# Storing and reloading split weights for the second half of the tokens in a hybrid RWKV-7 / S5 layer

## The chip, the cores and the metric

The kernel runs on one core of one Trainium2 chip. The metric is the device time of one execution in microseconds (us). Three runs of the kernel before gave a median of 1566.11 us (1561.93 to 1569.23). One more execution was recorded by the hardware profiler; all views of the profile are of that one.

## What is computed

One layer of a decoder trunk, in float32, for 1024 tokens of width 1024. The first sub-layer mixes tokens by two branches in parallel, an RWKV-7 recurrence and an S5 state-space scan, and merges them by learned gates:

```python
gates = sigmoid(h @ w_in[..., gate columns] + b_gate); g_rwkv, g_s5 = split(gates, 2)
# S5 branch, its last step
y = gelu(y); y = y * sigmoid(y @ w_glu + b_glu)
# merge of the branches, output projection, residual
o_rwkv = rwkv7_branch(...) @ w_branch_rwkv        # 512 -> 1024
o_s5   = s5_branch(...)    @ w_branch_s5          # 512 -> 1024
mixed  = (g_rwkv * o_rwkv + g_s5 * o_s5) @ w_out  # 1024 -> 1024
x = x + rms_norm(mixed, norm_mix_post)
```

The second sub-layer is a gated MLP with a short convolution. The change does not touch it.

## The kernel before

**Three matmuls for one.** TensorE multiplies in a rounded float32 type. To keep accuracy, each operand is split into a rounded part (names that end in `h`: `wh`, `hh`) and the remainder (`wl`, `hl`), and `mm3_steps` (L163) makes three matmuls for each 128x128 block of weights: `wh`·`xh`, `wh`·`xl`, `wl`·`xh` (L173, L174, L175). Activations are 128 features by 512 tokens, so the tokens fall in two halves, first and second (`th` 0 and 1 in the code).

**Weights.** `load_w` (L144) loads a 128x512 tile of weights into `wf` (L156, 256 KB, issued on SyncE's queue), rounds it into `wh` on ScalarE (L157), and takes the remainder into `wl` on VectorE (L158). There are two `wf` buffers and four each of `wh` and `wl` in rotation. So the load of a tile waits until the tile two before has been rounded and subtracted, and the rounding of a tile waits until TensorE is done with the tile four before. A weight of 512 inputs (`w_glu`, `w_br`) is one such tile; one of 1024 inputs (`w_out`, `w_up`) is two.

**The merge.** For either half of the tokens there are 4 tiles of `w_glu` (`glu_tile`, L1073), 16 of `w_br` (`gate`, L1084; for each block of 128 outputs one tile for RWKV and one for S5) and 16 of `w_out` (`outproj`, L1215): 36 tiles. `glu_tile` reads the S5 output `YU` again for its last product (L1064, packets of 256 bytes); `gate` reads the stored gates `GT` (L1088) and multiplies them with the matmul result on VectorE (L1091). For the first half this work (`merge`, `outproj(0)`) is background work, which `drive` (L186) puts between the steps of the RWKV recurrence. For the second half, `merge_s5` does the four `glu` tiles and the S5 gates, `merge_rk` the RWKV gates and the sums, and `outproj(1)` the projection. Beside the latter runs `mid_norms(0)`: the first half's post-norm (L1202, L1203, with `x` loaded again into `tx`, L1194), the stores of the sum (`X`, L1206), its squares, and the pre-norm of the MLP (L1252).

**Order.** TensorE's instructions stay in the order in which the code emits them. On all other engines and on SyncE's queue a scheduler orders them by priority and by its own estimate of when each is ready; `load_w` has a high priority (`HPW`). Each engine, and SyncE's queue too, then runs its list strictly in that order: an instruction that waits holds up all behind it.

Of the kernel before, what the change touches and what calls it, by code (L numbers as in the profile page):

```python
# [9 lines left out]
F32 = mybir.dt.float32  # L10
# [61 lines left out]
class Kern:  # L72
# [68 lines left out]
            V.scalar_tensor_tensor(y, h, 1.5, y, ALU.add, ALU.mult)  # L141
        return y

    def load_w(self, *srcs, pool=None):  # L144

        nc = self.nc
        wh, wl = [], []
        wp = pool or self.wp
        with self.tc.high_priority(HPW):
            for src in srcs:  # L150
                for o in range(0, src.shape[1], 512):
                    n = min(512, src.shape[1] - o)
                    h = wp.tile([128, 512], F32R, tag="wh", name=self.nm("wh"), bufs=4 if pool else NWH)
                    l = self.lx() if pool else wp.tile([128, 512], F32R, tag="wl", name=self.nm("wl"), bufs=NWL)
                    f = self.wp.tile([128, 512], F32, tag="wf", name=self.nm("wf"), bufs=NWF)
                    nc.sync.dma_start(f[:, :n], src[:, o:o + n])  # L156
                    nc.scalar.copy(h[:, :n], f[:, :n])  # L157
                    nc.vector.tensor_tensor(l[:, :n], f[:, :n], h[:, :n].bitcast(F32), ALU.subtract)  # L158
                    wh.append(h)
                    wl.append(l)  # L160
        return wh, wl

    def mm3_steps(self, ps, w, wk, xh, xl):  # L163
# [909 lines left out]
    def glu_tile(self, m, xs, t, y, to):  # L1073

        nc = self.nc
        w = self.load_w(self.a["w_glu"][m])
        ps = self.gmp()
        yield from self.mm3_steps(ps, w, 0, [x[0] for x in xs], [x[1] for x in xs])
        t3 = t.rearrange("p (n j) -> p n j", j=8)
        nc.scalar.activation(t, ps, AF.Tanh, bias=self.hb["b_glu"][:, m:m + 1], scale=0.5)  # L1080
        nc.vector.scalar_tensor_tensor(t3, t3, 1.0, y(), ALU.add, ALU.mult)
        self.split_half(*to, t)

    def gate(self, j, m, th, br, t, out):  # L1084

        nc = self.nc
        w = self.load_w(self.a["w_br"][j, m])
        nc.sync.dma_start(t, self.GT[8 * j + m][:, th * 512:th * 512 + 512])  # L1088
        ps = self.gmp()
        yield from self.mm3_steps(ps, w, 0, [b[0] for b in br], [b[1] for b in br])  # L1090
        nc.vector.scalar_tensor_tensor(out, t, 1.0, ps, ALU.add, ALU.mult)  # L1091
# [123 lines left out]
    def outproj(self, th, mg, mx):  # L1215

        nc, hp = self.nc, self.hp[th]
        for m in range(NK):
            w = self.load_w(self.a["w_out"][m])
            ps = self.gmp()  # L1220
            yield from self.mm3_steps(ps, w, 0, [x[0] for x in mg], [x[1] for x in mg])
            y = hp.tile([128, 512], F32, tag=f"hl{m}", name=self.nm("mx"), bufs=1)
            nc.scalar.copy(y, ps)
            mx.append(y)
            sq = hp.tile([128, 512], F32, tag=f"hh{m}", name=self.nm("sq"), bufs=1)
            nc.scalar.activation(sq, y, AF.Square)
            if m:
                nc.vector.tensor_tensor(sq, sq, self.acc[th], ALU.add)
            self.acc[th] = sq
# [479 lines left out]
    def front_half(self):  # L1709

        tc = self.tc
        self.h = [None, None]
        self.now = self.credit = 0.0
        self.pause, self.fill_prio, self.acc = False, HPW, {}
        self.mark, self.chained = False, False
        self.s5_in_done, self.stored, self.mixed_in, self.open = -1, None, False, 0
        with tc.tile_pool(name="lxp", bufs=4) as self.lxp, tc.tile_pool(name="s5c", bufs=1) as self.s5c, \
                tc.tile_pool(name="u8p", bufs=1) as u8p, tc.tile_pool(name="eva", bufs=NEVA) as self.evp, \
                tc.tile_pool(name="psx", bufs=1, space=PSUM) as self.psx:
            self.ps, self.ngm = self.psx, 4  # L1720
            self.u8 = [u8p.tile([128, 8, 128], F32, name=f"u8_{b}") for b in range(4)]
            with tc.tile_pool(name="xp", bufs=1) as xp:
                with tc.high_priority(HPN):
                    xs = [self.load_x(0, xp)]
                    self.setup()
                    self.s5w = {}
                    self.s5_load(0)
                    self.s5_load(1)
                    for _ in self.norm(0, xs[0], xp):
                        pass  # L1730
                    xs.append(self.load_x(1, xp))
                self.fill = [self.s5_in(xp), self.mix_in()] + [self.gate_tiles(m) for m in range(14)] + [
                    self.merge_loads(), self.gate_tiles(14, 15)]
                self.outs, self.yr = 0, []
                self.drive([(HPN, self.norm(1, xs[1], xp))])
                self.drain(lambda: self.stored == 3)
                with tc.high_priority(HP):
                    self.s5_setup()
            with tc.tile_pool(name="s5p", bufs=1) as self.s5p:
                self.s5d = [{} for _ in range(4)]  # L1740
                self.tabs = self.s5_done = -1
                self.drive([(HP, self.s5_lane()), (HP, self.tab_lane())])
                self.drain(lambda: self.mixed_in and not self.open)
        self.early_stack = ExitStack()
        self.rka = self.early_stack.enter_context(tc.tile_pool(name="rka", bufs=1, side="right"))
        with tc.tile_pool(name="rk", bufs=1) as self.rk, tc.tile_pool(name="evb", bufs=NEV) as self.evp, \
                tc.tile_pool(name="psy", bufs=1, space=PSUM) as self.psx:
            self.ps, self.ngm = self.psx, 2
            self.rwkv_setup()
            self.ds = [{} for _ in range(4)]  # L1750
            self.nat = self.prep = self.chains = -1
            self.fronts = 0
            mg, self.mx0 = [], []
            self.drive([(HP, self.prep_lane(0)), (HP, self.prep_lane(1)), (HP2, self.chain_lane()), (HP2, self.out_lane(mg))])
            self.drain(lambda: self.mark)
# [148 lines left out]
```

## Time and profile before

| | |
|---|---|
| median of three runs | 1566.11 us (1561.93 to 1569.23) |
| profiled execution, its own time | 1569.72 us |
| its span in the trace | 1566.6 us |
| TensorE busy | 1490.2 us, 95% of the span, mean granted clock 0.977 |
| VectorE busy | 1127.4 us, 72% |
| ScalarE busy | 691.0 us, 44% |
| DMA | 213.84 MB, 137 GB/s over the span |

A page of the profile gives busy times of engines, the groups of instructions that cost most, and the DMA issues with the time from issue to landing. "PE" is TensorE, "DVE" VectorE, "ACT" ScalarE, "POOL" GpSimd, "SPq" SyncE's DMA queue. In a row of the timeline stand the start in us, the duration in us, the engine, the line, the operation, what it writes and reads, and in brackets how long the engine was idle before it and what ended that. A table of windows gives the busy time of PE, its weight loads, DVE, ACT and POOL for each stretch of the span, the granted clock (1.00 is full speed), the mean busy share of the 16 DMA engines, and what they moved in GB/s. In the second half of the tokens the `glu` tiles start near 757 us, the S5 gates at 770 us, the RWKV gates at 802.6 us and the projection at 824.4 us, which ends near 881 us.

### The profile page before, as it was taken

What the parts mean: (1) busy time and instruction counts of PE and PEld (TensorE: products, weight loads), DVE (VectorE), ACT (ScalarE), POOL (GpSimd) and SP (SyncE); (2) the same over time, 40 slices, a digit from 0 to 9 for tenths busy, and PEclk for the clock granted to TensorE, in tenths of its full rate; (3) what the DMA queues carried; (4) which work ended last, traced back from release to release, by engine and by line L of the source; (5) the groups of instructions that cost most, each with busy time, mean ns of one, the idle gap of its engine ahead of it and who ended that gap; (6) DMA issues with size and microseconds to landing.
All of it is one profiled execution on the core that took longest, in us unless ns stands there. A gap on an engine that the chain in (4) does not pass through costs nothing.

```text
span 1566.6 us, 26064 instructions
## 1 busy us (share of the span) xinstructions
PE 1490.2 (95%) x10028; PEld 1194.1 (76%) x10028; DVE 1127.4 (72%) x1963; ACT 691.0 (44%) x1115; POOL 164.2 (10%) x218
## 2 busy tenths in 40 slices
PE   5999899999999999999998999999999999999995
PEld 4787788787777776667686888788888887888784
DVE  6798784664465656875586689877777777698777
ACT  5354442224243345565433445444445444443451
POOL 2120000415224142100000000000000000000000
PEclk9999999999999989999898999999999999999997
DMA  6164243344335256552854343322222225943712
GB/s 210 41 201 124 85 126 124 110 137 145 109 116 159 84 172 169 142 163 79 264 189 158 133 165 135 114 88 81 82 81 81 81 84 197 321 171 121 241 68 107
DMA packets 133420, 213.84 MB, mean 137 GB/s; under 512 B 38656, under 2 KB 44800, under 8 KB 133296
## 3 DMA queue, kind: packets, MB, share of 16 engines
q1 hardware_dynamic: 124208, 188.32, 36.4%
q0 software_dynamic: 7936, 21.77, 4.7%
q10 hardware_dynamic: 1152, 2.10, 0.3%
q8 instruction: 78, 1.28, 0.3%
q14 instruction: 46, 0.38, 0.1%
HBM read 156.56 MB, written 53.48 MB: 134 GB/s over the span
## 4 chain that ended last, share of the span: by engine, by line
PE 71%; DVE 14%; DMA 7%; issue 4%; ACT 3%; SPq 1%; POOL 1%; DVEq 0%; ACTq 0%; POOLq 0%
PE gm L173 9%; PE gm L174 8%; PE gm L175 8%; PE rp L1344 4%; PE rp L1345 4%; PE rp L1346 4%; DMA st<-in_w_down_dram 2%; PE ch L173 2%; PE ch L174 2%; PE mm L174 2%; PE mm L1346 2%; PE mm L1345 2%; PE ch L175 2%; PE mm L1344 2%; PE mm L173 2%
## 5 line engine op out<-in xcount | busy, mean ns | idle before, releaser
L173 PE MATMUL gm<-hh,wh 128*128 128x512 f32 x688 | 294.1, 428 | 5.5 <-ACT hh L227 2.1
L174 PE MATMUL gm<-hl,wh 128*128 128x512 f32 x688 | 273.1, 397 | 0.4 <-DVE hl L228 0.4
L175 PE MATMUL gm<-hh,wl 128*128 128x512 f32 x656 | 259.9, 396 | 0.0
L157 ACT CAST wh<-wf 128x512 fp32r<-128x512 f32 x179 | 110.8, 619 | 209.7 <-PE gm L174 125.7
L158 DVE TENSOR_TENSOR wl<-wf,wh 128x512 fp32r<-128x512 f32 x175 | 123.9, 709 | 97.5 <-ACT wh L157 82.7
L173 PEld LDWEIGHTS gm<-hh,wh 128*128 128x128 f32 x688 | 131.3, 191 | 42.4 <-issue 4.3
L174 PEld LDWEIGHTS gm<-hl,wh 128*128 128x128 f32 x688 | 131.8, 192 | 23.8 <-issue 1.4
L175 PEld LDWEIGHTS gm<-hh,wl 128*128 128x128 f32 x656 | 125.0, 191 | 28.1
L1519 PE MATMUL d<-xl,wh 128*128 128x512 f32 x308 | 120.9, 393 | 3.4 <-DVE xl L228 3.4
L1518 PE MATMUL d<-xh,wh 128*128 128x512 f32 x308 | 120.7, 392 | 2.1 <-ACT xh L227 2.1
L1520 PE MATMUL d<-xh,wl 128*128 128x512 f32 x308 | 120.6, 392 | 0.0
L1344 PE MATMUL rp<-t,h 128*128 128x512 f32 x216 | 84.4, 391 | 1.4 <-ACT p L1358 1.4
L1346 PE MATMUL rp<-t,l 128*128 128x512 f32 x216 | 84.2, 390 | 0.5 <-DVE l L228 0.5
L1345 PE MATMUL rp<-t,h 128*128 128x512 f32 x216 | 84.1, 389 | 0.0
L1519 PEld LDWEIGHTS d<-xl,wh 128*128 128x128 f32 x308 | 58.2, 189 | 17.0 <-DVE xl L228 5.1
L1518 PEld LDWEIGHTS d<-xh,wh 128*128 128x128 f32 x308 | 58.2, 189 | 14.6 <-ACT xh L227 2.4
L1520 PEld LDWEIGHTS d<-xh,wl 128*128 128x128 f32 x308 | 58.1, 189 | 12.1
L227 ACT CAST h<-r 128x1024 fp32r<-128x1024 f32 x34 | 35.8, 1054 | 61.1 <-PE rp L1345 32.5
L228 DVE TENSOR_TENSOR l<-r,h 128x1024 fp32r<-128x1024 f32 x34 | 41.6, 1225 | 29.3 <-ACT h L227 27.8
L1365 DVE SCALAR_TENSOR_TENSOR y<-zv,vecs,y 128x1023 f32<-128x1023 f32 (+1 forms) x36 | 46.1, 1281 | 8.6 <-ACT y L1363 8.6
L1344 PEld LDWEIGHTS rp<-t,h 128*128 128x128 f32 x216 | 40.5, 188 | 10.8 <-ACT p L1358 2.2
L1346 PEld LDWEIGHTS rp<-t,l 128*128 128x128 f32 x216 | 40.5, 188 | 9.3 <-DVE l L228 1.0
(442 smaller groups left out, 3373.0 us busy)
## 6 DMA issues: line engine op xcount, KB each, us to landing
r<-in_w_up_dram SPq DMA_DIRECT2D x36, 512.0 KB, 3.2
wf<-in_w_in_dram SPq DMA_DIRECT2D x68, 256.0 KB, 2.7
st<-in_w_down_dram SPq DMA_DIRECT2D x55, 256.0 KB, 4.3
st<-ACT SPq DMA_DIRECT2D x44, 256.0 KB, 4.5
wf<-in_w_up_dram SPq DMA_DIRECT2D x36, 256.0 KB, 2.8
ACT<-y POOLq DMA_DIRECT2D x18, 512.0 KB, 2.9
GT<-ev SPq DMA_DIRECT2D x32, 256.0 KB, 2.1
wf<-in_w_br_dram SPq DMA_DIRECT2D x32, 256.0 KB, 3.1
```

The source lines that it names most:

```text
L157: nc.scalar.copy(h[:, :n], f[:, :n])
L158: nc.vector.tensor_tensor(l[:, :n], f[:, :n], h[:, :n].bitcast(F32), ALU.subtract)
L173: mm(ps, a, xh[k], start=k == 0, stop=False)
L174: mm(ps, a, xl[k], start=False, stop=False)
L175: mm(ps, b, xh[k], start=False, stop=k == n - 1)
L1344: mm(ps, wh[:, c], xh, start=first and k == 0, stop=False, skip_group_check=True)
L1345: mm(ps, wh[:, c], xl, start=False, stop=False, skip_group_check=True)
L1346: mm(ps, wl[:, c], xh, start=False, stop=k == 3, skip_group_check=True)
L1365: V.scalar_tensor_tensor(y[:, lag:], z[:, 0:1024 - lag], self.vec(nme, i), y[:, lag:], ALU.mult, ALU.add)
L1518: mm(ps, wh[:, c], xh[:, x], start=start, stop=False, skip_group_check=True)
L1519: mm(ps, wh[:, c], xl[:, x], start=False, stop=False, skip_group_check=True)
L1520: mm(ps, wl[:, c], xh[:, x], start=False, stop=stop, skip_group_check=True)
```

## The change

When a tile of `w_glu`, `w_br` or `w_out` is made for the first half of the tokens, `wh` and `wl` are also stored to DRAM (256 KB each). The stores are issued by the next call of `load_w`. When the same tile is asked for again, both parts are loaded straight into `wh` and `wl`, and neither `wf` nor the rounding nor the subtraction is there.

```diff
-    def load_w(self, *srcs, pool=None):
+    def load_w(self, *srcs, pool=None, key=None):
...
+        new = []
         with self.tc.high_priority(HPW):
             for src in srcs:
                 for o in range(0, src.shape[1], 512):
                     n = min(512, src.shape[1] - o)
                     h = wp.tile([128, 512], F32R, tag="wh", name=self.nm("wh"), bufs=4 if pool else NWH)
                     l = self.lx() if pool else wp.tile([128, 512], F32R, tag="wl", name=self.nm("wl"), bufs=NWL)
+                    wh.append(h)
+                    wl.append(l)
+                    if (key, o) in self.kept:
+                        for t, d in zip((h, l), self.kept[key, o]):
+                            nc.sync.dma_start(t[:, :n].bitcast(F32), d[:, :n])
+                        continue
                     f = self.wp.tile([128, 512], F32, tag="wf", name=self.nm("wf"), bufs=NWF)
                     nc.sync.dma_start(f[:, :n], src[:, o:o + n])
                     nc.scalar.copy(h[:, :n], f[:, :n])
                     nc.vector.tensor_tensor(l[:, :n], f[:, :n], h[:, :n].bitcast(F32), ALU.subtract)
-                    wh.append(h)
-                    wl.append(l)
+                    if key is not None:
+                        self.kept[key, o] = [self.dram.tile([128, 512], F32, name=self.nm("kw")) for _ in range(2)]
+                        new += zip((h, l), self.kept[key, o])
+            for t, d in self.keeping:
+                nc.sync.dma_start(d, t.bitcast(F32))
+            self.keeping = new
         return wh, wl
...
-        w = self.load_w(self.a["w_glu"][m])
+        w = self.load_w(self.a["w_glu"][m], key=("glu", m))
...
-        w = self.load_w(self.a["w_br"][j, m])
+        w = self.load_w(self.a["w_br"][j, m], key=("br", j, m))
...
-            w = self.load_w(self.a["w_out"][m])
+            w = self.load_w(self.a["w_out"][m], key=("out", m))
...
+        self.kept, self.keeping = {}, []
```

Lines behind L144 move down by up to 12. TensorE's list of instructions is the same; the lists of SyncE's queue, ScalarE and VectorE differ. The first place is SyncE's queue where the second half's `glu` tiles give way to the first S5 gates. Before (`wf` are weights of the first S5 gates; `YU_107` to `YU_110` are the four blocks of S5 output that the four `glu` tiles multiply at their end):

```order
L156 DMA wf_8639<-in_w_br_dram 128x512
L1194 DMA tx_8659<-in_x_dram 128x512
L1064 DMA et_8478<-YU_107 128x8x64
L156 DMA wf_8695<-in_w_br_dram 128x512
L1064 DMA et_8507<-YU_108 128x8x64
L156 DMA wf_8769<-in_w_br_dram 128x512
L1175 DMA t_1543_8601<-YR_114 128x512
L1064 DMA et_8536<-YU_109 128x8x64
L156 DMA wf_8792<-in_w_br_dram 128x512
L1064 DMA et_8565<-YU_110 128x8x64
```

The same place now (`kw` are the stored parts; the four pairs are the weights of the first four S5 gates):

```order
L160 DMA wh_8745<-kw_7428 128x512
L160 DMA wl_8746<-kw_7429 128x512
L1075 DMA et_8620<-YU_107 128x8x64
L160 DMA wh_8771<-kw_7495 128x512
L160 DMA wl_8772<-kw_7496 128x512
L1075 DMA et_8647<-YU_108 128x8x64
L160 DMA wh_8825<-kw_7576 128x512
L160 DMA wl_8826<-kw_7577 128x512
L160 DMA wh_8897<-kw_7655 128x512
L160 DMA wl_8898<-kw_7656 128x512
L1075 DMA et_8674<-YU_109 128x8x64
L1075 DMA et_8701<-YU_110 128x8x64
```

Each of the pairs waits until TensorE is done with the tile four before, which are the `glu` tiles 0 to 3; `YU_109` and `YU_110` now stand behind all four pairs, and the fourth `YR` and several `tx` have moved further down.

The second place is the same queue around the last three RWKV gates and the first tiles of `w_out` (`GT_80`, `GT_81`, `GT_82` are the gates of RWKV blocks 5, 6 and 7). Before:

```order
L156 DMA wf_9104<-in_w_out_dram 128x512
L156 DMA wf_9143<-in_w_out_dram 128x512
L1194 DMA tx_9564<-in_x_dram 128x512
L156 DMA wf_9149<-in_w_out_dram 128x512
L1088 DMA t_1651_9015<-GT_80 128x512
L156 DMA wf_9205<-in_w_out_dram 128x512
L1194 DMA tx_9566<-in_x_dram 128x512
L156 DMA wf_9211<-in_w_out_dram 128x512
L1088 DMA t_1658_9042<-GT_81 128x512
L156 DMA wf_9303<-in_w_out_dram 128x512
L1088 DMA t_1665_9069<-GT_82 128x512
```

Now:

```order
L160 DMA wl_9205<-kw_7965 128x512
L1099 DMA t_1706_9125<-GT_80 128x512
L1205 DMA tx_9636<-in_x_dram 128x512
L160 DMA wh_9241<-kw_8061 128x512
L160 DMA wl_9242<-kw_8062 128x512
L1205 DMA tx_9638<-in_x_dram 128x512
L160 DMA wh_9245<-kw_8069 128x512
L160 DMA wl_9246<-kw_8070 128x512
L1099 DMA t_1712_9150<-GT_81 128x512
L160 DMA wh_9299<-kw_8176 128x512
L160 DMA wl_9300<-kw_8177 128x512
L1099 DMA t_1718_9175<-GT_82 128x512
```

`GT_80` stood behind the fourth tile of `w_out` and a `tx`, now behind the second tile; `GT_81` stood behind the sixth, now behind the fourth; `GT_82` stood behind the seventh, now behind the fifth.

The third place is SyncE's queue at the start of the first half's merge, now:

```order
L170 DMA kw_6735<-wh_6729 128x512
L170 DMA kw_6736<-wl_6730 128x512
L163 DMA wf_6849<-in_w_br_dram 128x512
L1036 DMA GT_89<-ev_6409 128x512
L170 DMA kw_6796<-wh_6790 128x512
L163 DMA wf_6909<-in_w_glu_dram 128x512
L170 DMA kw_6797<-wl_6791 128x512
L1099 DMA ev_6643<-GT_75 128x512
```

Before, the `wf` loads and the `GT` and `YU` transfers followed one another there without the `kw` rows. A store of a tile stands next to the load two tiles on.

## The prediction

> **What bounds the kernel now.** I read the page first: TensorE is busy 95% of the span, and the rounding and subtraction of weights cost much on two engines that are not.
>
> ```profile
> PE 1490.2 (95%) x10028; PEld 1194.1 (76%) x10028; DVE 1127.4 (72%) x1963; ACT 691.0 (44%) x1115; POOL 164.2 (10%) x218
> L157 ACT CAST wh<-wf 128x512 fp32r<-128x512 f32 x179 | 110.8, 619 | 209.7 <-PE gm L174 125.7
> L158 DVE TENSOR_TENSOR wl<-wf,wh 128x512 fp32r<-128x512 f32 x175 | 123.9, 709 | 97.5 <-ACT wh L157 82.7
> ```
>
> The change takes away 36 of each: 36 x 0.619 = 22.3 us of ScalarE and 36 x 0.709 = 25.5 us of VectorE. They count only where TensorE waits for these engines. So next comes the table of windows by stage: the first half's merge under the recurrence (590 to 690) and its projection (690 to 745), then of the second half the `glu` tiles (745 to 790), the gates (790 to 824), the start of the projection (824 to 846) and its rest; and two stretches where DMA is heaviest.
>
> ```profile
> core 0: us, PE busy (x) PEld busy (x) DVE busy (x) ACT busy (x) POOL busy (x), PEclk, DMA share, GB/s
> 590.00:690.00 100.00, 94.10 (x1234) 67.47 (x1233) 77.57 (x180) 56.31 (x116) 15.09 (x26) 0.98 0.61 169
> 690.00:745.00 55.00, 54.61 (x560) 40.59 (x560) 31.17 (x69) 27.60 (x65) 0.00 (x0) 1.00 0.26 87
> 745.00:790.00 45.00, 41.27 (x160) 31.48 (x159) 25.89 (x48) 19.71 (x34) 0.00 (x0) 0.85 0.76 244
> 790.00:824.00 34.00, 34.00 (x152) 28.15 (x151) 32.39 (x53) 14.01 (x24) 0.00 (x0) 1.00 0.63 204
> 824.00:846.00 22.00, 15.81 (x52) 11.44 (x50) 11.37 (x28) 6.00 (x10) 0.00 (x0) 0.69 0.35 120
> 846.00:882.00 36.00, 36.00 (x164) 29.96 (x163) 22.45 (x35) 18.60 (x34) 0.00 (x0) 1.00 0.45 154
> 755.00:760.00 5.00, 4.97 (x22) 3.77 (x21) 2.16 (x4) 2.66 (x5) 0.00 (x0) 1.00 0.91 324
> 1325.00:1335.00 10.00, 7.95 (x29) 6.13 (x27) 9.83 (x10) 4.00 (x6) 0.00 (x0) 0.83 0.94 317
> ```
>
> TensorE sets the pace nearly everywhere. VectorE is full from 790 to 824 (32.39 of 34) without holding TensorE, and the bill comes at 824, where idle time and a reduced clock stand together. Near 770 it is the same on a smaller scale. Only these two places have something to win.
>
> ```profile
> 824.15 0.39 PE L175 MATMUL ch<-t,wl 128*128 128x512 f32 x1
> 827.55 0.39 PE L175 MATMUL mm<-t,wl 128*128 128x512 f32 x1
> 829.69 0.49 PE L173 MATMUL mm<-t,wh 128*128 128x512 f32 x1 [1.76 <-ACT t L232]
> 831.44 1.71 PE L246 MATMUL rp<-ones,tm 128*128 128x1 f32 x8
> 836.57 0.79 PE L173 MATMUL mm<-t,wh 128*128 128x512 f32 x1 [3.43 <-ACT t L232]
> 839.29 0.79 PE L173 MATMUL mm<-t,wh 128*128 128x512 f32 x1 [0.77 <-ACT t L232]
> 844.86 0.40 PE L175 MATMUL ch<-e,wl 128*128 128x512 f32 x1
> ```
>
> From 824.15 to 827.55 five steps of three matmuls take 3.40 us, 0.68 each: that is full speed, and a tile of four steps takes 2.72. From 824.38 (T) to 845.09 twelve steps and eight small matmuls are done. They need 12 x 0.68 + 0.9 = 9.1 us (the small ones took 1.71 at the reduced clock, about half of that at full speed) and took 20.7: 11.6 us are lost, of which the brackets show 6.0 as idle, and 5.6 go to the reduced clock and what it drags out. What was late? SyncE's queue issued the last three gates late, held behind `wf` loads that wait for VectorE's subtraction:
>
> ```profile
> 822.38 0.41 SPq L1088 DMA_DIRECT2D t<-GT  x1
> 828.78 0.42 SPq L1088 DMA_DIRECT2D t<-GT  x1
> 831.38 0.43 SPq L1088 DMA_DIRECT2D t<-GT  x1
> 826.49 0.69 DVE L1091 SCALAR_TENSOR_TENSOR t<-t,ch 128x512 f32<-128x512 f32 x1 [1.59 <-DMA t<-GT]
> 827.69 0.69 DVE L158 TENSOR_TENSOR wl<-wf,wh 128x512 fp32r<-128x512 f32 x1
> 833.18 0.16 DVE L266 TENSOR_SCALAR rv<-rp 128x4 f32<-128x4 f32 x1 [2.21 <-PE rp L246]
> 837.16 0.68 DVE L1091 SCALAR_TENSOR_TENSOR t<-t,ch 128x512 f32<-128x512 f32 x1
> ```
>
> The second gate left 0.4 us after the subtraction that ended at 828.38; the first took 4.1 us to arrive.
>
> **The change part by part.** *End of the merge (824 to 846).* The three gates now stand behind reloads that wait for TensorE alone, not for VectorE. `GT_80` leaves when the sixth RWKV gate's matmuls are done (T - 5.4) and two issues, at T - 4.6; it lands 4.1 us later, so step 5 of the first output block (steps count from 0 to 7), at T + 3.4, no longer waits. The eight small matmuls end at T + 6 x 0.68 + 0.9 = T + 5.0 and the norm's L266 starts there. `GT_81` leaves at T + 0.8, lands at T + 4.9, in time. From L266 to the last gating took 833.18 to 837.16, 4.0 us, and from there to step 7 on TensorE 839.29 - 837.16 = 2.1. `GT_82` waits for the first tile of `w_out` (T + 2.7), lands by T + 7.7 and is no longer last. So step 7 starts at T + 5.0 + 4.0 + 2.1 = T + 11.1 instead of T + 14.9: **-3.8 us**, if the clock falls as before. Bounds: 0 (another load is late in their place) and -3.8 - 5.6 = -9.4 (the clock stays up).
>
> *Start of the S5 gates (757 to 790).* Here the change adds a wait. `YU_109` and `YU_110` now stand behind the fourth reload, which waits for the last `glu` tile.
>
> ```profile
> 767.83 0.39 PE L173 MATMUL gm<-e,wh 128*128 128x512 f32 x1
> 767.85 0.38 SPq L1064 DMA_DIRECT2D et<-YU  x1
> 771.42 0.62 ACT L1065 ACTIVATE et<-et 128x512 f32<-128x512 f32 x1
> 774.00 0.80 PE L173 MATMUL mm<-e,wh 128*128 128x512 f32 x1 [1.27 <-ACT e L232]
> 776.35 0.79 PE L173 MATMUL mm<-e,wh 128*128 128x512 f32 x1 [0.40 <-ACT e L232]
> DMA to landing us min/median/max: 2.9/3.8/5.1
> ```
>
> The last row is that of the four `et<-YU` here. That tile's last step starts at 767.83 and is over at 768.7; two issues later, at 769.5, `YU_109` leaves (before: 767.85), lands at 773.3, and 2.6 us later (774.00 - 771.42) TensorE takes it: 775.9, or 2 us late. `YU_110` and the step after follow in ScalarE's and VectorE's order by as much. Behind them the gates' first steps and all of TensorE wait. **+2.0 us**; bounds 0 (a landing at 2.9 and casts out of ScalarE's way) and +3.3 (5.1 instead of 3.8).
>
> *Gates (780 to 824).* By the new order twelve pairs of weights, sixteen other loads on SyncE's queue and eight stores on ScalarE's stand between the reload for the fifth S5 gate and that for the last RWKV gate: 48 x 0.262 = 12.6 MB in eleven tiles, 30 us. The two heavy windows give 324 / 0.91 = 356 and 317 / 0.94 = 337 GB/s at a full share; at 340 the bytes take 37 us, 7 too many. Cover: a reload is issued when TensorE is done with the tile four before, three tiles (8.2 us) ahead of its use; it lands in about 3.5 (two issues and a landing of 3.1, below), so some 4.7 us of backlog are hidden. Lower bound 0, since the eight stores may trail; upper 7 - 4.7 = 2.3, and with a fall of the clock 2.3 + 5.6 = 7.9. I take **+1.5**, nearest to the bound without a fall, since nothing idles there now.
>
> The Trainium skill ("DMA: Bandwidth & Descriptors", Specifications) puts a core's share of HBM at about 358 GB/s. By it the estimate would be 35 us for these bytes and the term 0.5; the heavy windows agree with it roughly.
>
> *First half (590 to 745).* 72 stores of 256 KB, 18.9 MB. Issue costs SyncE two times 0.3 to 0.4 us per tile, beside tiles of 4 us and more. The loads that they stand beside wait for the same subtraction, so no new wait arises in the queue. Buffers are stored long before TensorE frees them. What is left is traffic:
>
> ```profile
> wf<-in_w_br_dram SPq DMA_DIRECT2D x32, 256.0 KB, 3.1
> st<-ACT SPq DMA_DIRECT2D x44, 256.0 KB, 4.5
> ACT hh L227 <- DMA ld<-YR: 3.8, 2, 3.0
> ACT et L1065 <- DMA et<-YU: 3.2, 3, 1.9
> DVE hl L1091 <- DMA ev<-GT: 0.9, 1, 0.9
> 659.95 4.63 DMA et<-YU
> 670.78 3.88 DMA et<-YU
> ```
>
> From 690 on the share is 0.26, and there is room. From 590 to 690 some 20 tiles are made: 10.5 MB, 105 GB/s. At 0.63 / 204 per GB/s (790 to 824) that is +0.32 on a share of 0.61, 0.93 in all, as in the stretch after 1325, where the `st<-ACT` loads run. These land in 4.5 us, against 3.1 for weights: I take +2 us per landing that is waited for. Two stand in the chain of waits (the last two rows), one more held VectorE for 0.9: 2 x 2 + 0.5 = **+4.5**. Bounds: -3.2 (the `et<-YU` loads are moved further down in the new order, and ScalarE's 3.2 us of waiting for them go) and +12 (two us on each of the six landings that the rows of waits, from 555 to 745, count).
>
> *Rest of the projection (846 to 882):* reloads of 512 KB per 2.72 us are 193 GB/s, where 154 were moved with half of that; TensorE has no gap: 0.
>
> **Sum:** 4.5 + 2.0 + 1.5 - 3.8 = +4.2. On the profiled execution's own time of 1569.72 us that is 1573.9. The median of the runs is 3.6 us lower than that execution, so 1570.3.
>
> **Rivals.** *The clock stays up (faster).* If the idle pieces left near 824 (2.3 us before step 6 and before step 7) are too short to bring the clock down, that term is -9.4; with the first half at -1 by the moved `YU` loads, +1 at 770 and nothing at the gates the sum is -9.4: 1557. In the gates VectorE sheds these subtractions (window, DVE busy, granted clock, DMA share, GB/s):
>
> ```profile
> 790.00:831.00 41.00, 10.14 (x15) 0.99 0.65 214
> ```
>
> For it: with fifteen of them gone VectorE is no longer 10 us behind at 824. Against it: the clock was already reduced at 830.4 (matmuls of 0.63 to 0.8 us) after 1.76 us of idling. The Trainium skill ("TensorE: Matmul & The Clock Gate", Why this matters for your kernels) asks only that gaps stay under about 3 us, by which this rival would hold; the row at 829.69 speaks against that.
>
> *Reloads come late (slower).* From 780 the DMA engines fall behind by more than the cover of 4.7 us; TensorE waits, and the clock falls: 7.9 instead of 1.5, 1576.7. It decides from the tile at which a reload lands over 8.2 us after its issue. For it: 37 us of transfers in 30. Against it: the stores may trail.
>
> *The stores congest the first half (slower).* All six landings are late, 12, and one gap brings the clock down, 5.6: 17.6 instead of 4.5, 1583. For it: the share of 0.93, and small packets. Against it: VectorE, not DMA, ends most waits there.
>
> **How the numbers follow.** A measurement of this kernel can tell about 0.5%, 7.8 us, from no change: 1558.3 to 1573.9. The forecast that costs and gain nearly cancel has 0.42, with a range of its own of 1562 to 1577 (0.36 within 0.5%, 0.06 slower); the clock that stays up 0.27 (0.25 faster, 0.02 within); late reloads 0.13; congestion 0.18. So faster 0.25, same 0.38, slower 0.37. The range of 8 in 10 takes in the rivals' prices: 1555 to 1588.
>
> **What would show it.** After: L157 and its subtraction 36 fewer each; VectorE below 28 of 34 us in the gates; step 7 of the first output block about 11 us after the last RWKV gate; the first S5 gate's last steps 2 us later than now against the `glu` tiles; DMA share above 0.85 from 590 to 690 and the first half's merge 4 to 5 us longer. It is wrong if TensorE waits for `wh<-kw` anywhere for over 2 us, if the gates still leave behind VectorE, or if the first half does not lengthen.

## The result, and the profile after

The changed kernel takes 1576.55 us (median of 7 runs, 1571.17 to 1582.68) beside 1563.83 us of the kernel before on the same chip: a ratio of 1.008, 95% interval 1.0053 to 1.0108. It is slower by 0.8%, some 12.5 us. Ratios leave out one execution, of run e7 below, that took 2924.98 us. Its profiled span is 1580.9 us, 14.3 more than before.

The page first: engines, the two groups that the change thins out, and the landing of the reloads (last number, us).

```profile
PE 1496.8 (95%) x10028; PEld 1198.8 (76%) x10028; DVE 1104.4 (70%) x1927; ACT 671.4 (42%) x1079; POOL 164.5 (10%) x218
L164 ACT CAST wh<-wf 128x512 fp32r<-128x512 f32 x143 | 88.6, 619 | 171.5 <-PE gm L185 114.6
L165 DVE TENSOR_TENSOR wl<-wf,wh 128x512 fp32r<-128x512 f32 x139 | 98.7, 711 | 85.0 <-ACT wh L164 70.2
wh<-kw SPq DMA_DIRECT2D x36, 256.0 KB, 4.4
```

The casts and subtractions fell by 36 each, VectorE by 23.0 us and ScalarE by 19.6, and the kernel is slower. Where? TensorE runs the same 10028 matmuls in the same order, so the start of the same matmul can be set against its start before. It is 0.8 us later at 600 us (times of before), 8.5 at 666, 9.7 at 757, 14.2 at 786, 14.2 at 824 and 14.1 at 846, and then stays there. The stages by windows, each moved by this lag:

```profile
core 0: us, PE busy (x) PEld busy (x) DVE busy (x) ACT busy (x) POOL busy (x), PEclk, DMA share, GB/s
590.00:696.50 106.50, 96.75 (x1237) 68.44 (x1235) 74.02 (x176) 54.40 (x114) 15.07 (x26) 0.97 0.79 238
696.50:754.60 58.10, 54.63 (x560) 40.53 (x560) 35.22 (x75) 29.89 (x68) 0.00 (x0) 1.00 0.71 236
754.60:804.20 49.60, 41.96 (x160) 32.48 (x159) 18.82 (x36) 13.29 (x22) 0.00 (x0) 0.83 0.82 264
804.20:838.20 34.00, 34.00 (x152) 28.16 (x151) 26.70 (x43) 8.36 (x14) 0.00 (x0) 1.00 0.98 341
838.20:860.10 21.90, 16.00 (x51) 11.41 (x50) 7.58 (x21) 3.10 (x5) 0.00 (x0) 0.69 0.52 192
815.00:825.00 10.00, 10.00 (x46) 8.29 (x45) 4.18 (x7) 1.61 (x3) 0.00 (x0) 1.00 1.04 387
```

The first stage takes 106.5 us in place of 100 and the second 58.1 in place of 55, the third 49.6 in place of 45. The gates take 34 as before, with TensorE full, though the DMA engines now move 341 GB/s; the end of the merge takes 21.9 us in place of 22, at the same reduced clock.

**First half.** The view of waits from 555 to 760 us (total, times, longest) has rows that before were absent or under a microsecond:

```profile
DVE hl L1102 <- DMA ev<-GT: 8.9, 3, 3.3
PE cz L852 <- DVE S L873: 5.7, 6, 2.3
DVE ld L909 <- DMA ld<-bv: 5.2, 2, 2.8
PE gm L184 <- DVE hl L1102: 4.2, 2, 3.4
```

The timeline shows how a late load reaches TensorE, in three places:

```profile
608.91 0.42 SPq L1099 DMA_DIRECT2D ev<-GT  x1
618.50 0.69 DVE L1102 SCALAR_TENSOR_TENSOR hl<-ev,gm 128x512 f32<-128x512 f32 x1 [2.83 <-DMA ev<-GT]
619.82 0.33 SPq L163 DMA_DIRECT2D wf<-in_w_glu_dram  x1
621.53 0.62 ACT L164 CAST wh<-wf 128x512 fp32r<-128x512 f32 x1 [4.00 <-DMA wf<-in_w_br_dram]
625.01 0.34 PE L852 MATMUL cz<-S,ar 64*64 64x64 f32 x8 [2.26 <-DVE S L873]
...
663.37 0.42 SPq L1099 DMA_DIRECT2D ev<-GT  x1
668.39 0.69 DVE L1102 SCALAR_TENSOR_TENSOR hl<-ev,gm 128x512 f32<-128x512 f32 x1 [3.30 <-DMA ev<-GT]
669.13 0.50 PE L184 MATMUL gm<-hh,wh 128*128 128x512 f32 x1 [3.38 <-DVE hl L1102]
...
700.54 0.42 SPq L908 DMA_DIRECT2D ld<-bv  x1
706.62 0.69 DVE L909 TENSOR_TENSOR ld<-ld,ld 128x512 f32<-128x512 f32 x1 [2.39 <-DMA ld<-bv]
708.16 0.54 PE L852 MATMUL cz<-S,ar 64*64 64x64 f32 x16 [1.83 <-DVE S L873]
```

Near 618 the first gate load lands 9.5 us after its issue. VectorE works its list in order: it holds the state update `S` of the recurrence, which is TensorE's own critical work, behind the product that waits for `GT`; the next subtraction comes late too, and with it the next `wf` load. At 669 the same happens with a load that now stands one weight load further back, at 706 with `bv`, which left at 675 us before.

**Start of the S5 gates.** What the second half's beginning waits for:

```profile
761.41 0.41 SPq L908 DMA_DIRECT2D ld<-TG  x1
767.41 0.69 DVE L909 TENSOR_TENSOR ld<-ld,ld 128x512 f32<-128x512 f32 x1 [3.84 <-DMA ld<-TG]
771.26 0.32 SPq L1186 DMA_DIRECT2D t<-YR  x1
776.36 0.62 ACT L238 CAST t<-t 128x512 fp32r<-128x512 f32 x1 [5.92 <-DMA wh<-kw]
777.62 0.50 PE L184 MATMUL gm<-e,wh 128*128 128x512 f32 x1 [2.47 <-ACT et L1091]
785.12 0.79 PE L184 MATMUL mm<-e,wh 128*128 128x512 f32 x1 [4.49 <-ACT et L1091]
```

The last `TG` load stands behind the first pair of reloads. Its product is stored as `YR` at 768.13; `t<-YR`, issued at 771.26, reads this back; and the cast of `t` stands in ScalarE's list ahead of the evacuation of a `glu` tile (L1091) for which TensorE waits. (The bracket at 776.36 names `wh<-kw`, the DMA that ended last by the profile; a cast from `t` to `t` needs `t<-YR`.)

**End of the merge.** The gate loads again:

```profile
836.70 0.32 SPq L1099 DMA_DIRECT2D t<-GT  x1
841.52 0.43 SPq L1099 DMA_DIRECT2D t<-GT  x1
842.02 0.69 DVE L1102 SCALAR_TENSOR_TENSOR t<-t,ch 128x512 f32<-128x512 f32 x1 [5.02 <-DMA t<-GT]
853.47 0.79 PE L184 MATMUL mm<-t,wh 128*128 128x512 f32 x1 [1.62 <-ACT t L243]
```

VectorE, no longer behind, sits idle for 5.02 us until the first of them arrives. The last row is step 7 of the first output block. It starts 15.1 us after the last matmul of the last RWKV gate (838.33), exactly as before (839.29 - 824.15). What held the first of the gate loads is a row of the waits of SyncE's queue from 790 to 846 us (total, times, longest):

```profile
SPq L1099 <- DMA tx<-in_x_dram: 1.5, 1, 1.5
```

The load needs nothing of that `tx`. It leaves at 836.70, as the `tx` lands that left eight transfers earlier (830.98, 5.70 us to land), counted over SyncE and ScalarE. From 790 to 846 us SyncE's queue waits 13.3 us in all for landings, 2.5 before; some 10 us of the 13.3 end with the landing of the transfer seven or eight places ahead. So a load can wait here for a transfer that it does not need, and the order of the list alone does not show it.

### The profile page after: what moved, and what is told of

It reads as the page before. It is cut to its first block, busy times and chain, and to the rows that moved or that the text cites. A ratio compares the mean times of both kernels' runs of the same rounds, so it can differ in the third digit from the quotient of the medians.

```text
span 1580.9 us, 26129 instructions
## 1 busy us (share of the span) xinstructions
PE 1496.8 (95%) x10028; PEld 1198.8 (76%) x10028; DVE 1104.4 (70%) x1927; ACT 671.4 (42%) x1079; POOL 164.5 (10%) x218
## 5 line engine op out<-in xcount | busy, mean ns | idle before, releaser
L184 PE MATMUL gm<-hh,wh 128*128 128x512 f32 x688 | 295.0, 429 | 10.2 <-DVE hl L1102 4.2
L164 ACT CAST wh<-wf 128x512 fp32r<-128x512 f32 x143 | 88.6, 619 | 171.5 <-PE gm L185 114.6
L165 DVE TENSOR_TENSOR wl<-wf,wh 128x512 fp32r<-128x512 f32 x139 | 98.7, 711 | 85.0 <-ACT wh L164 70.2
L1531 PEld LDWEIGHTS d<-xh,wl 128*128 128x128 f32 x308 | 58.2, 189 | 12.1
```

Source lines behind the costliest of these rows:

```text
L184: mm(ps, a, xh[k], start=k == 0, stop=False)
L1531: mm(ps, wl[:, c], xh[:, x], start=False, stop=stop, skip_group_check=True)
```

## The experiments

All kernels have TensorE's 10028 matmuls in the same order, so one table serves for all: how much later TensorE becomes in each stretch (us of the kernel before; one profiled execution of each; minus is time gained), the sum at 1549 us, and the ratio of the medians with its interval. What stands up to 600 is mostly luck of the clock: before stands at half clock for 10.2 us from 571 us, the others for 0 to 10.2. Each row is one execution: behind 882 us, after the last tile that any of the edits touches, the lags still move by -2.5 to 2.3 us (most of the column "rest"), so a single figure of that size can be chance.

| kernel | to 600 | 600-666 | 666-757 | 757-786 | 786-824 | 824-846 | rest | sum | ratio |
|---|---|---|---|---|---|---|---|---|---|
| the change | 0.8 | 7.8 | 1.2 | 4.4 | 0.0 | -0.1 | 0.4 | 14.5 | 1.0080 (1.0053-1.0108) |
| e1 stores alone | -2.1 | 7.8 | 0.4 | 2.3 | 0.6 | -1.5 | 0.2 | 7.8 | 1.0069 (1.0042-1.0095) |
| e2 reloads alone | 0.8 | 0.6 | -0.6 | 0.5 | 1.0 | -2.4 | 0.9 | 0.8 | 1.0007 (0.9989-1.0025) |
| e3 stores by GpSimd | -1.4 | 2.0 | 21.0 | 5.3 | 0.3 | -2.4 | -2.5 | 22.3 | 1.0152 (1.0128-1.0176) |
| e4 w_out only | -1.9 | 0.0 | -0.3 | 0.8 | 0.7 | -2.1 | -0.3 | -3.0 | 1.0001 (0.9980-1.0022) |
| e5 thin stores | -1.3 | 3.4 | 4.0 | -0.1 | 0.0 | -0.9 | -0.1 | 5.1 | 1.0048 (1.0030-1.0065) |
| e6 stores low | -2.3 | 0.5 | 7.4 | 5.4 | 2.7 | 0.8 | 2.3 | 16.8 | 1.0113 (1.0094-1.0133) |
| e7 eight gate loads | -2.3 | 0.1 | -0.3 | 4.2 | 0.0 | -3.9 | 0.9 | -1.3 | 1.0014 (1.0001-1.0027) |
| e8 e4 and e7 | 1.6 | 0.0 | -0.6 | 7.9 | 0.7 | -4.5 | 0.4 | 5.4 | 1.0039 (1.0026-1.0051) |
| e9 loads high | -4.8 | -1.2 | 8.8 | 8.3 | 0.0 | -5.0 | 0.2 | 6.3 | 1.0068 (1.0051-1.0086) |
| e10 its control | -1.5 | -2.5 | 5.2 | -0.8 | 0.0 | 1.9 | 1.9 | 4.1 | 1.0018 (1.0003-1.0033) |
| e11 three gate loads | -3.3 | 0.1 | 0.4 | -0.1 | 0.0 | -1.0 | 0.8 | -2.9 | 0.9990 (0.9981-0.9999) |
| e12 e4 and e11 | -1.1 | -1.4 | -0.5 | 1.5 | 0.6 | -2.3 | -1.4 | -4.6 | 0.9993 (0.9978-1.0008) |

### The two halves apart

Stores alone:

```diff
-                    if (key, o) in self.kept:
+                    if False:
...
-                    if key is not None:
+                    if key is not None and (key, o) not in self.kept:
```

> The 72 stores of the first half stay, the second half makes its weights again from the inputs. Theory (the loss is mostly the first half, 9.4 of 14 us in the changed kernel's trace, from landings that grow and from loads that the stores push down SyncE's queue): 9 us slower than the kernel before, the projection of the first half ends 9 us later than before, and nothing is added behind it. Rival (stores are hidden under TensorE, the loss comes from the reloads): 0 to 3 us slower.

Reloads alone:

```diff
+                        if len(self.kept) < 4:
...
+                        else:
+                            self.kept[key, o] = list(self.kept.values())[len(self.kept) % 4]
```

> Only the first four tiles are stored; all 36 pairs of the second half are loaded, each from one of these four, so the weights of the second half are not the reference's; bytes and issues of the second half are those of the change. Theory: the first half as before; the second half's start loses 2 to 5 us by what SyncE's queue does around the first reloads, the end gains nothing: 2 to 5 us slower than before. Rival (the reloads themselves come late): over 7 us slower, with TensorE waiting for weights between the S5 gates and the projection. Rival (the reloads pay where stores do not disturb): 4 us faster or more.

The stores alone cost 1.0069, nearly all of the change; the first half loses 8.2 us (600 to 757) as the change does with 9.0. The reloads alone cost nothing that can be told. TensorE's weight loads wait for them 0.8 us in all, and the stretch from 786 to 824 loses 1.0. So both rivals about the reloads fall, and so do the 2 to 5 us that were expected of them. The start of the S5 gates loses 2.3 with stores and no reload, 0.5 with reloads and next to no stores, 4.4 with both. In e2, where it loses 0.5, both `TG` loads stand ahead of the first reload, and `YU_109` and `YU_110` behind the same four pairs as in the change: their later place is not what costs. e5 below has both `TG` loads ahead of the first reload too, and loses nothing there (-0.1).

### Bytes or places

Stores from another queue:

```diff
-                nc.sync.dma_start(d, t.bitcast(F32))
+                nc.gpsimd.dma_start(d, t.bitcast(F32))
```

> The same stores and reloads, but the stores are issued by GpSimd, so that SyncE's queue keeps the loads of the first half in nearly the order of the kernel before. Order theory (the later places of GT and bv loads make the two later steps of the first half's loss, 4.5 and 2.4 us): the first half loses 2 to 5 us in place of 9.4, and the whole is 5 to 9 us slower than before. Traffic theory (the bytes alone): the first half loses 8 to 10 us whoever issues the stores, and the whole is 12 to 14 us slower.

Until 666 us the first half loses 2.0 in place of 7.8, with all the bytes (600 to 660: 245 GB/s at a share of 0.76, beside TensorE at 56.72 of 60). That speaks for the places. Then it loses 21 at once, and neither theory had this. GpSimd's queue, too, has transfers on the critical chain. First the kernel before, then this one; `mt<-md` feeds the inverse on VectorE, `gr<-xd` brings it back:

```profile
604.52 2.12 POOL L759 DMA_DIRECT2D mt<-md  x4 [0.46 <-DMA md<-gr]
```

```profile
606.76 0.56 POOL L770 DMA_DIRECT2D mt<-md  x1 [3.89 <-DMA md<-gr]
621.15 0.56 POOL L770 DMA_DIRECT2D mt<-md  x1
665.87 0.54 POOL L170 DMA_DIRECT2D kw<-wl  x1 [1.79 <-DVE x L782]
666.43 1.29 POOL L785 DMA_DIRECT2D xd<-x  x2
680.96 0.43 DVE L804 STREAM_TRANSPOSE ld<-gr 32x256 f32<-32x256 f32 x1 [13.24 <-DMA gr<-xd]
681.53 0.28 PE L811 MATMUL cz<-ld,gr 32*32 32x32 f32 x2 [12.89 <-DVE ld L804]
```

Four loads that went out in 2.12 us now take from 606.76 to 621.15, because between them stand stores that wait for casts and subtractions; at the end TensorE has nothing else to do and waits 12.89 us.

Thin stores (the weights of the second half as in e2):

```diff
+                            thin = [self.dram.tile([128, 8], F32, name=self.nm("kw")) for _ in range(2)]
+                            new += zip((h[:, :8], l[:, :8]), thin)
```

> As in the run with reloads alone (the weights of the second half come from four stored tiles and are not the reference's), but each of the other 64 stores of the first half is there with 8 columns of 512: 4 KB in place of 256 KB. The stores stand on SyncE's queue with their waits, the bytes are gone; loads keep some of the places that they have in the change, though the scheduler puts the YU and bv loads earlier. Queue-wait theory (a store that waits for its cast or subtraction holds up the loads behind it): the first half still loses 5 to 9 us, the whole is 6 to 10 us slower than before. Bytes theory (what delays the loads are the bytes of the stores ahead of them): the first half loses 0 to 2 us, the whole is 0 to 3 us slower.

With 8 whole stores and 64 of 4 KB, 2.4 MB in place of 18.9, the first half still loses 7.4 us. So most of the bytes are not needed for the loss. The step near 624, though, it cannot tell apart: its eight whole stores stand just there, and the first gate load lands in 9.4 us, as in the change. Nor can e2 settle it: the same eight stores, and the gate load landed in 7.5 us and the stretch lost 0.6.

Stores with the lowest priority:

```diff
+            self.tc.cur_priority += 1000000
             for t, d in self.keeping:
                 nc.sync.dma_start(d, t.bitcast(F32))
+            self.tc.cur_priority -= 1000000
```

> All 72 stores and all reloads, on SyncE's queue as in the change, but the stores are given to the scheduler with the lowest priority, so that GT, YU, bv and wf loads keep nearly the places of the kernel before and the stores fill in between. Place theory (loads moved behind stores make the loss): the first half loses 0 to 4 us in place of 9.4, the start of the S5 gates 0 to 2 in place of 5.4, the whole is 0 to 5 us slower than before. Traffic theory: the first half still loses 8 us or more, the whole is 10 us slower or more.

Up to 666 the loss is gone (0.5), as the place theory has it, and not for want of bytes. By 660 us as many stores have left as in the change (26), and from 600 to 660 us more is moved (first row: the change, second: e6):

```profile
600.00:660.00 60.00, 56.07 (x689) 38.77 (x690) 45.23 (x124) 30.33 (x69) 8.41 (x15) 0.97 0.76 233
600.00:660.00 60.00, 57.32 (x771) 41.32 (x771) 49.04 (x133) 32.05 (x73) 10.19 (x18) 0.97 0.83 248
```

But none leaves from 660 to 669, then 22 up to 710 us (17 in the change), and it is lost behind: 7.4 up to 757 and 5.4 at the S5 gates, where ScalarE waits 7.8 us at the cast of `t`, 5.9 in the change. The whole is worse than the change. So the place theory falls. The traffic theory comes within 0.1 us of its figure for the first half (7.9, it said 8 or more) and has that for the whole (1.13%, it said 10 us or more), though up to 666, with more traffic than in the change, nothing was lost.

Loads above weights and stores, and the same in the kernel before (the same two lines around the issue of `GT`, `YU`, `bv`, `TG`, `YR` and its store):

```diff
+        self.tc.cur_priority -= 1000000
         nc.sync.dma_start(t, self.GT[8 * j + m][:, th * 512:th * 512 + 512])
+        self.tc.cur_priority += 1000000
```

> The change with all its bytes, but the loads that TensorE's neighbours wait for (GT, YU, bv, TG, YR and its store) are given to the scheduler with a priority above the weights and the stores, so that they no longer stand behind stores or reloads. Place theory: the step near 624 (4.5 us) and the two of bv and TG (2.4 near 700, 2.5 to 5 near 765) go, the whole is 0 to 5 us slower than before. Bytes theory: what the loads gain in place they lose in the rings behind 18.9 MB of stores, the whole is still 10 us slower or more.

> The control for it: the kernel before with the same loads above the weights, no stores and no reloads. If the places that these loads have in the kernel before already cost something (the 11.6 us at the end of the merge, the idle time near 770), it is 3 to 8 us faster than before; if they cost nothing, within 2 us. What the change costs when places are equal is the difference between this run and the one with the change.

The waits from 590 to 775 us, of e9 and then of e10:

```profile
ACT wh L164 <- DMA wf<-in_w_br_dram: 7.3, 3, 4.0
ACT t L238 <- DMA wl<-kw: 6.6, 1, 6.6
DVE ld L911 <- DMA ld<-bv: 2.9, 1, 2.9
DVE hl L1110 <- DMA ev<-GT: 2.9, 2, 2.2
```

```profile
ACT wh L157 <- DMA wf<-in_w_br_dram: 5.9, 3, 2.9
DVE hl L1099 <- DMA ev<-GT: 0.7, 1, 0.7
```

The waits for `GT` and `bv` shrink (8.9 to 2.9 for `GT`), and ScalarE now waits for the weights. (The row `t <- wl<-kw` is again the cast of `t`, which needs `t<-YR`.) e10, without any store, shows that this order by itself costs 2.7 us from 600 to 757; e9 loses 7.6 there, 4.9 more. It looks as if the loss moves to whichever loads stand last. The place theory, with 0 to 5 us for the whole, falls; e9 is 1.0068, 10.7 us, which is what the bytes theory said. By the ratios it is 0.5% slower than its control, some 8 us, where the change is 0.8% slower than the kernel before.

Taken together: that the stores make the loss is shown (e1, e2). Up to 666 us it is their places in SyncE's queue more than their bytes, for e3 and e6 move as much and lose 2.0 and 0.5 us in place of 7.8. Over the whole, places and bytes are not told apart: e5 has an eighth of the bytes and still 1.0048, but e6 and e9, with the stores out of these loads' way, have 1.0113 and 1.0068. Each order that was tried made some load late that VectorE or ScalarE has next in its list.

### The end of the merge

Only `w_out` kept (the calls for `w_glu` and `w_br` without `key`):

> Only w_out is stored and reloaded (16 tiles, 32 stores, 32 loads). Theory: the stores fall behind the first half's merge, where the DMA engines are a quarter busy, so the first half loses under 1.5 us; no reload stands among the glu tiles and S5 gates, so nothing is lost there; the end of the merge gains at most what an earlier gate load gives: the whole between 4 us faster and 1 us slower, no change that can be told. Rival (the price is in the reloads near the end): 4 us slower or more.

No change that can be told, as expected: the stores cost nothing where the DMA engines had been a quarter busy, and in the trace 2.1 us are gained at the end.

Gate loads from GpSimd, in the kernel before, and in e4:

```diff
-        nc.sync.dma_start(t, self.GT[8 * j + m][:, th * 512:th * 512 + 512])
+        (nc.gpsimd if th and not j else nc.sync).dma_start(t, self.GT[8 * j + m][:, th * 512:th * 512 + 512])
```

> The kernel before with one thing moved: the eight GT loads of the second half's RWKV gates are issued by GpSimd, which has nothing else there, and no longer by SyncE behind wf loads. Theory of the prediction (at the end of the merge 11.6 us are lost because these loads leave late): step 7 of the first output block comes 10 to 11 us after the last RWKV gate in place of 14.9, and the whole is 4 to 9 us faster. Rival (VectorE, full from 790 to 824, is itself behind; the loads are only the last of several things that are late): 0 to 2 us faster, with the same clock stretch near 830.

> Only w_out is stored and reloaded, and the eight GT loads of the second half's RWKV gates are issued by GpSimd. With the loads early and eight or so subtractions less for VectorE before step 7, the theory expects the end of the merge to keep 5 to 9 us of its 11.6, and the first half to lose under 1.5 us: 4 to 9 us faster than before. Rival (the bytes of 32 stores and 32 reloads cost what is gained, or the clock falls all the same): within 2 us of the kernel before.

Neither is faster. The end gains 3.9 and 4.5, but 4.2 and 7.9 are lost ahead of it: GpSimd sends all eight at once, in e7 from 750 us on, into the busiest stretch, where a `t<-YR` that leaves at 751.63 lands only 8.6 us later (row of e7; the eighth follows at 754.71):

```profile
750.70 3.83 POOL L1088 DMA_DIRECT2D t<-GT  x7 [93.04 <-DMA wf<-in_w_glu_dram]
```

So only the last three were moved, and held back, in the kernel before and in e4:

```diff
-        nc.sync.dma_start(t, self.GT[8 * j + m][:, th * 512:th * 512 + 512])
+        if th and not j and m >= 5:
+            nc.gpsimd.tensor_copy(t[:, :1], self.first[m - 0][:, :1])
+            nc.gpsimd.dma_start(t, self.GT[8 * j + m][:, th * 512:th * 512 + 512])
+        else:
+            nc.sync.dma_start(t, self.GT[8 * j + m][:, th * 512:th * 512 + 512])
```

> The kernel before with only the last three GT loads of the second half's RWKV gates issued by GpSimd, each held by a copy of one column of an S5 gate's result, so that they leave between 800 and 810 us, behind the traffic near 760 and ahead of the end of the merge. Theory (late gate loads cost the end of the merge some 4 us, which the run with eight loads gained there and lost near 760): the end of the merge 3 to 5 us shorter, nothing lost elsewhere, the whole 3 to 5 us faster. Rival (VectorE's backlog keeps the end as it is): within 1.5 us.

> Only w_out is stored and reloaded, and the last three GT loads of the RWKV gates leave from GpSimd between 795 and 805 us. Theory (the end of the merge has two limits that hide each other: gate loads that leave late, and VectorE that is behind with subtractions and the norm; the run with early loads alone kept 1 us of it, the change alone 0.6): with both eased the end of the merge is 4 to 5 us shorter than in the kernel before, the start of the S5 gates costs 0 to 3 us as in the run with w_out alone, and the whole is 1 to 5 us faster. Rival (each gain is taken up by the next wait): within 1 us of the kernel before.

In e11 the last of the three leaves at 803.86 and lands at 808.2, 25 us ahead of its use, and nothing is lost near 760; yet the end gains 1.0 only, where 3 to 5 were expected. Rows of e11 and then of e9, the gates' window of each and step 7:

```profile
803.86 0.55 POOL L1090 DMA_DIRECT2D t<-GT  x1 [0.30 <-POOL t L1089]
787.20:821.20 34.00, 34.00 (x152) 28.16 (x151) 31.42 (x52) 14.12 (x24) 3.33 (x6) 1.00 0.68 221
835.40 0.79 PE L173 MATMUL mm<-t,wh 128*128 128x512 f32 x1 [0.82 <-ACT t L232]
```

```profile
801.00:835.00 34.00, 34.00 (x151) 28.16 (x150) 27.96 (x44) 8.19 (x13) 0.00 (x0) 1.00 0.98 348
845.39 0.80 PE L184 MATMUL mm<-t,wh 128*128 128x512 f32 x1 [3.32 <-ACT t L243]
```

From the last RWKV gate's last matmul to step 7 it is 15.1 us before and in the change, 14.0 in e11 (loads early, VectorE at 31.42 of 34), 13.0 in e4 (VectorE partly relieved, loads 2 us earlier), 12.3 in e2 (VectorE relieved, loads 1 to 4 us earlier), 12.1 in e12 (loads early, VectorE partly relieved) and 10.1 in e9 (845.39 - 835.24; VectorE relieved, loads 3 to 6 us earlier). So late loads and VectorE's backlog each have a part. That the two hide each other, as was expected of e12, is not shown: its 3.0 us are what e11 and e4 gain apart (1.1 and 2.1), and its end is 2.3 us shorter in the table, not 4 to 5. Nor do the shortest ends price the place, for in e7, e8 and e9 (11.9, 10.6 and 10.1) TensorE had come 4, 8 and 8 us later into the stretch, and that may have given VectorE time to catch up.

No version is clearly faster than the kernel before: e11 has 0.9990 (up to 0.9999), e12 0.9993 (up to 1.0008), where 1 to 5 us were expected.

## Why the prediction was right and wrong

The prediction said 1570, between 1555 and 1588, with 0.37 for slower. The time was inside, and slower as the sum had it, but the sum was a third of what came: 4.2 us against some 14 in the traces. That it fell inside owes more to the range, made wide for the prices of the rivals, than to the account, and is luck so far: two terms were short by 7 us together, a gain of 3.8 did not come, and neither did a cost of 1.5. The rival of late reloads named 1576.7, nearly the time that was measured, and what it describes did not occur.

**First half (+4.5, came 9.0 from 600 to 757).** The direction was right, and landings grew (the first gate load from 6.2 to 9.5 us). The share was 0.79 over the stretch, below the 0.93 of the working. The step that failed is the sentence "The loads that they stand beside wait for the same subtraction, so no new wait arises in the queue". It weighs what a store itself waits for, and not where the stores move the loads: a gate load stands one weight load further back and holds TensorE for 3.4 us at 669, `bv` leaves at 700 in place of 675 us. The later place of `ld<-bv` and of that gate load could be read in the order and was not priced; nor was what holds behind them, since VectorE's list has TensorE's `S` right behind. e5, with 2.4 MB of stores, still loses 7.4: so most of what the prediction put down to traffic alone was not traffic. The congestion rival had the right place and an amount of 12, but named landings alone.

**Start of the S5 gates (+2.0, came 4.4).** Mis-sized, and for another reason than the one given. The prediction followed `YU_109` and `YU_110`. e2 has them in the same place and loses 0.5. What came was `TG`, `YR`, `t<-YR` and the cast that stands in ScalarE's list ahead of TensorE's evacuations, a chain of which the prediction has nothing; the order ahead of it shows only that "the fourth `YR` and several `tx` have moved further down".

**Gates (+1.5, came 0.0).** The lower bound was right: the cover of 4.7 us held, though the landings of `wh<-kw` were 4.4 and not 3.1. The late reloads did not occur. The Trainium skill ("DMA: Bandwidth & Descriptors", Specifications) has about 358 GB/s as a core's share of HBM; here the 34 us ran at 341, and ten of them, mixed loads and stores, at 387, so for this mix the figure is no ceiling.

**End of the merge (-3.8, came -0.1).** The failed step is "`GT_80` leaves when the sixth RWKV gate's matmuls are done". It left at 836.70, 1.6 us before the last gate's last matmul and 2.7 later than predicted; the last 1.5 us of this it waited for the landing of an earlier `tx`, a wait that the prediction does not have, and it landed in 5.2 us, not in 4.1, behind a stretch with a share of 0.98. Some of the gain was there to be had: e2, with the same reloads and next to no stores, has step 7 at 12.3 us from that matmul, where the prediction's T + 11.1 would be 11.3. That the 11.6 us were lost for late loads was part of the cause: in e11 the loads are early and 1.0 us is gained, with VectorE still at 31.42 of 34 in the gates, which the prediction had noticed ("VectorE is full") and not priced. The clock fell here again, for 13.65 us as before, so the rival in which it stays up fell with it.

**What it said would show it wrong.** TensorE nowhere waits for `wh<-kw`, VectorE is below 28 of 34 (26.70), and the first half lengthens: so none of these showed it wrong. Two of the signs that it named for being right did not come: step 7 was 15.1 us after the last RWKV gate, not about 11, and the DMA share from 590 to 690 was 0.78, not above 0.85. None of the signs watched for loads that move.

Open: how much of the step near 624 us is bytes and how much is place (the same load landed in 9.5 us in the change and 9.4 in e5, which lose there, and in 7.5 in e2 and 7.9 in e6, which do not), how places and bytes share the loss behind 666 us, and how the first half would run with a queue that has room, since GpSimd's has not.

## What to carry to other kernels

A transfer added to an in-order queue costs what the loads behind it then make late, and their users' lists in turn: read each moved load against the engine that waits for it, and not only the bytes against the bandwidth. Work that is redone off the critical path (36 casts and subtractions, 42.6 us of two engines) may be cheaper than storing it, for the stores fall where the other data is needed. And where two things are late at one place, what easing one of them gains does not price the place: here one gave 1.0 us, the other 2.1 and both together 2.3.

## What the runs showed of the hardware

With loads and stores mixed in 256 KB transfers the DMA engines moved 387 GB/s over 10 us while TensorE had no gap. The Trainium skill ("Perfetto Trace Analysis", Engine Utilization, Roofline) says that a single active core can pull more than 358 GB/s, up to about 435; the trace agrees.

All stretches at half clock between 100 and 1500 us, in all fourteen traces, last 3.41 us or a multiple of it (23.9 in e3). In the changed kernel one of 3.41 us follows a wait of TensorE of 2.26 us at 625, another the wait of 3.38 at 669. The Trainium skill ("TensorE: Matmul & The Clock Gate", What's actually happening) has a free-running window of 3413 ns; the lengths agree, and the first of these two waits is shorter than one window.
